# Keys by Strassen's seven products: a change to the shared-key stage of an mLSTM and band-attention trunk

## The chip, the cores and the metric

The kernel runs on one core of one Trainium2 chip. The metric is the device time of one execution in microseconds (us); lower is better. The core has five instruction queues that matter here: PE (the matrix engine), DVE (vector), ACT (scalar), POOL, which does next to nothing in this kernel, and SP, which only issues DMA transfers. Each queue takes its instructions in the order in which the program lists them, and an instruction that waits for a semaphore holds up everything behind it in its own queue.

## What is computed

The input is 512 tokens of width 2048, in float32. Layer A is an mLSTM mixer, layer B an attention mixer; both have a modulated RMSNorm ahead and a gated residual behind. Between the two layers one set of keys and values is computed from the residual stream, and layer B reads it. Cut to what the change touches:

```python
kmod = sc @ kv_ada_w.astype(F32) + kv_ada_b.astype(F32)
hkv = modulate(rmsnorm(x, kv_g), kmod[:, :D_MODEL], kmod[:, D_MODEL:]).astype(x.dtype)
kv = hkv @ kv_w                                            # 512 x 2048 by 2048 x 4096
k_sh = kv[..., :B_WIDTH].reshape(Bn, S, B_HEADS, B_DH)     # 16 heads of 128 features
v_sh = kv[..., B_WIDTH:].reshape(Bn, S, B_HEADS, B_DH)
...
def band_attention_mixer(h, k, v, w_in, rel_table, w_out):
    qz = h @ w_in
    q = qz[..., :B_WIDTH].reshape(Bn, S, B_HEADS, B_DH)
    z = qz[..., B_WIDTH:]
    o = chunk_band_attention(q, k, v, rel_table)
    y = o.reshape(Bn, S, B_WIDTH) * jax.nn.silu(z.astype(F32))
    return y.astype(h.dtype) @ w_out
```

## The kernel before

All arithmetic is float32, made of float32r matmuls. `split` writes a high part of an operand with ACT (the cast, L153) and the rest with DVE (the subtraction, L154), and `mm3` then issues three matmuls for each product: high by high, high by low, low by high (all at L174). So a 128x128 weight block against 512 tokens is three matmuls of 512 columns.

The weights (520 pieces of 512 KB and some smaller) are laid out in DRAM in the order in which they are used. `wpiece` takes the next one: a DMA on SP into a buffer `wr`, ACT's cast into `wh`, DVE's subtraction into `wl`. The pool `wp` holds three buffers of each kind. So the DMA of piece i+3 waits until DVE is through with piece i, and ACT's cast of piece i+3 waits until PE is through with piece i.

The program is written as Python loops, and a planner sets the order of the instructions on each engine; parts under `tc.high_priority(AHEAD)` (the weight pieces above all) are put forward. The order that comes out is fixed in the built program.

The stages in order: start and layer A (to 1544 us in the profile), A's output projection `ps_y` (to 1896), and then the part that the change is about:

- `residual` and `turned` finish the residual stream, turn it to features x tokens and keep it in the DRAM scratch `nsc`. `key_input` makes the 16 tiles `hkv` (128 features x 512 tokens, high and low), the input of the key and value projections.
- `values(g, ms)`: 512 columns of the values for the token tiles `ms`, accumulated in PSUM tiles `ps_kv`, then copied by ACT into the SBUF tiles `kv[h]`. The column groups g = 0 and 1 are done first for token tiles 0 and 1, then for 2 and 3 (`PAIRS`).
- the keys, a loop over 16 feature tiles: `proj_a` accumulates `ps_k` over 16 blocks of k (48 matmuls of 512 columns), ACT copies it into `kv[i]`.
- `values(2)` and `values(3)` on all four token tiles.
- 16 tiles `h2`, the input of layer B: each is read back from `nsc` (`kept`, into a tile `xt` of the pool `tp`, six buffers), scaled on DVE (L704) and split on ACT and DVE. They take the buffers of the `hkv` tiles, which come free one after another during `values(3)`.
- 16 heads: `queries`, `weights`, `gated`, `flipped`, `mixed`. Each head has two projections of 48 matmuls, `ps_q` and `ps_z`. `mixed` splits the gated output into a tile `y2`.
- the output projection of B on the 16 tiles `y2` (`ps_y` again), and `finish`.

Of the kernel before, what the change touches and what calls it, by code (L numbers as in the profile page):

```python
# [15 lines left out]
P = 128  # L16
# [24 lines left out]

def stream():

    out = []

    def tile_a(mat, col, kts=KT):
        for k in range(0, kts, 8):
            out.append((mat, list(range(k, k + 8)), [(col, P)]))

    def tile_b(mat, col, kts=KT):  # L50
        for k in range(0, kts, 2):
            out.append((mat, [k, k + 1], [(col, 512)]))

    for k0, k1 in BLOCKS:
        for k in range(k0, k1):
            out.append(("a_w_in", [k], [(c, P) for c in LEAD]))
        for c in LATER:
            out.append(("a_w_in", list(range(k0, k1)), [(c, P)]))
# [16 lines left out]
    for i in range(KT):  # L75
        tile_a("kv_w", i * P)
# [10 lines left out]


def sizes():
    return [len(kts) * sum(n for _, n in cs) for _, kts, cs in stream()]  # L90
# [15 lines left out]
def hybrid_trunk(ctx, tc, xT, xN, c, adaT, cols, wst, wg, ext, kc, out):  # L106
# [5 lines left out]
    wp = ctx.enter_context(tc.tile_pool(name="wp", bufs=3))  # L112
# [4 lines left out]
    def pool(name, bufs=1):  # L117
        return tc.tile_pool(name=name, bufs=bufs, reuse_waits="tile")
# [6 lines left out]
    bsc = dram.tile([BH, P, EXTW], F32, name="bsc")  # L125

# [31 lines left out]
    def wpiece(mat):  # L158

        i, at = wpos  # L160
        m, kts, cs = order[i]
        assert m == mat
        n = len(kts) * sum(w for _, w in cs)
        wpos[:] = i + 1, at + P * n
        with tc.high_priority(ahead[0]):
            raw = wp.tile([P, 1024], F32, tag="raw", name=f"wr{i}")[:, :n]
            nc.sync.dma_start(raw, wst[at : at + P * n].rearrange("(p n) -> p n", p=P))
            hi = wp.tile([P, 1024], F32R, tag="hi", name=f"wh{i}")[:, :n]
            lo = wp.tile([P, 1024], F32R, tag="lo", name=f"wl{i}")[:, :n]
            split(hi, lo, raw)  # L170
        return hi, lo
# [23 lines left out]
    def proj_b(mat, xs, pss, ms=range(4), kts=KT, at={}, late=0):  # L195
# [3 lines left out]
        for k0 in range(0, kts, 2):  # L199
# [14 lines left out]
            held.clear()  # L214

# [344 lines left out]
    kp = kst.enter_context(pool("kp", bufs=KT))  # L560
    rst = ExitStack()
    rp = rst.enter_context(pool("rp", bufs=12))
    tst = ExitStack()
    tp = tst.enter_context(pool("t2", bufs=6))
# [3 lines left out]
    def y_tile(k):  # L568
        while len(ys) <= k:
            h, q = divmod(len(ys) // 2, 2)  # L570
            with tc.high_priority(AHEAD):
                raw = wp.tile([P, 2, S], F32, tag="raw", name=f"yr{h}_{q}")
# [128 lines left out]
    for k in range(KT):  # L701
# [6 lines left out]
        h2.append(t)  # L708
    tst.close()
    rst.close()  # L710
# [4 lines left out]
    y2 = []  # L715

    def queries(h):
        ps = newp(f"ps_q{h}")
# [61 lines left out]
    def mixed(h, pts, v, sz):  # L780
# [29 lines left out]
    for m in range(4):  # L810
        t = [xp.tile([P, 2, S], F32, tag="x", name=f"x2_{m}_{i}") for i in range(2)]
# [25 lines left out]
    kst.close()  # L837


def layouts(x, c, ada_w, ada_b, g_pre, g_post, a_w_in, a_conv_w, a_conv_b, a_gate_b, a_g_head,  # L840
# [3 lines left out]
    def cc(v):  # L844
# [15 lines left out]
            np.concatenate([mats[mat][k * P : (k + 1) * P, c0 : c0 + n] for k in kts for c0, n in cs], 1).ravel()  # L860
# [32 lines left out]
```

## Time and profile before

| | us |
|---|---|
| median of 3 runs (lowest to highest) | 2863.78 (2862.81 to 2864.45) |
| the profiled execution's own time | 2862.53 |
| its span, from first to last instruction | 2860.7 |
| PE busy | 2832.2 (99%) |
| DVE busy | 1587.4 (55%) |
| ACT busy | 1126.1 (39%) |
| keys, `ps_k` (768 matmuls) | 174.08 |
| `values(2)` and `values(3)`, `ps_kv` (384 matmuls) | 87.04 |

The page gives for each engine its busy time; the chain of waits follows the end of the program back to what released each step; the timeline lists instructions by start and duration. A matmul's duration is its own passage through the array. What counts in a run of matmuls is the distance from one start to the next, which is shorter, since they overlap.

### The profile page before, as it was taken

The page shows a single profiled execution, that of the slowest core. Times are in us where ns is not written, and L with a number is a line of the kernel's source. Part 1 is how long each engine was busy: PE and PEld are TensorE (multiplying, and loading weights), DVE is VectorE, ACT ScalarE, POOL GpSimd, SP SyncE. Part 2 cuts the span into 40 slices and gives each one's busy share as a digit, 9 for nine tenths or more (in the row PEclk, how much of TensorE's full clock was granted, in tenths as well). Part 3 has the DMA queues.
Part 4 walks back from the last instruction along what each step waited for, and adds up shares of the span by engine and source line. Part 5 has one row for each costly group of instructions (what it writes and reads, how often), then busy time and mean ns, then how long its engine had stood idle before and what let it go on. Part 6 is the DMA issues. An engine that isn't in the chain of part 4 may idle for free.

```text
span 2860.7 us, 33028 instructions
## 1 busy us (share of the span) xinstructions
PE 2832.2 (99%) x12770; PEld 2340.4 (82%) x12770; DVE 1587.4 (55%) x2358; ACT 1126.1 (39%) x1646; POOL 0.2 (0%) x4
## 2 busy tenths in 40 slices
PE   7999999999999999999999999999999999999998
PEld 5787888888888888888888888888888888888887
DVE  7986747466375564764735445575222455545425
ACT  4244524333242342332424345454222445545323
POOL 0000000000000000000000000000000000000000
PEclk9999999999999999999999999999999999999999
DMA  8874546456456464554635557786222322222334
GB/s 307 310 235 159 192 158 211 168 173 209 155 184 213 136 225 155 195 203 154 209 108 177 180 195 238 231 274 217 96 99 103 138 92 86 90 91 88 137 103 173
DMA packets 154950, 491.09 MB, mean 172 GB/s; under 512 B 17012, under 2 KB 26132, under 8 KB 154280
## 3 DMA queue, kind: packets, MB, share of 16 engines
q1 hardware_dynamic: 154792, 488.98, 50.2%
q8 instruction: 100, 1.64, 0.2%
q14 instruction: 58, 0.48, 0.0%
HBM read 467.89 MB, written 26.26 MB: 173 GB/s over the span
## 4 chain that ended last, share of the span: by engine, by line
PE 93%; DVE 3%; DMA 2%; issue 1%; ACT 1%; SPq 0%; DVEq 0%; ACTq 0%
PE ps_y L174 17%; PE ps_z L174 17%; PE ps_o L174 12%; PE ps_v L174 12%; PE ps_qk L174 9%; PE ps_q L174 6%; PE ps_k L174 6%; PE ps_kv L174 5%; PE ps_l L174 2%; PE ps_s L174 2%; PE ps_n L174 2%; PE ps_lead L174 1%; DVE wl L154 1%; DVE ada L245 1%; DMA wr<-in_wst 1%
## 5 line engine op out<-in xcount | busy, mean ns | idle before, releaser
L154 DVE TENSOR_TENSOR wl<-wr,wh 128x1024 fp32r<-128x1024 f32 (+3 forms) x586 | 680.4, 1162 | 1078.1 <-ACT wh L153 1077.6
L153 ACT CAST wh<-wr 128x1024 fp32r<-128x1024 f32 (+3 forms) x586 | 587.3, 1003 | 1433.0 <-PE ps_y L174 235.6
L174 PE MATMUL ps_y<-wh,y 128*128 128x512 f32 x1536 | 475.2, 390 | 0.0
L174 PE MATMUL ps_z<-h,wh 128*128 128x512 f32 x1408 | 433.9, 389 | 0.0
L174 PEld LDWEIGHTS ps_y<-wh,y 128*128 128x128 f32 x1536 | 288.2, 188 | 59.2
L174 PE MATMUL ps_v<-wh,h 128*128 128x512 f32 x1024 | 317.2, 389 | 0.0
L174 PEld LDWEIGHTS ps_z<-h,wh 128*128 128x128 f32 x1408 | 263.3, 188 | 54.0
L174 PE MATMUL ps_y<-wl,y 128*128 128x512 f32 x768 | 299.1, 389 | 0.0
L174 PE MATMUL ps_o<-h,wh 128*128 128x512 f32 x896 | 276.2, 389 | 0.0
L174 PE MATMUL ps_z<-h,wl 128*128 128x512 f32 x704 | 274.1, 389 | 0.0
L174 PE MATMUL ps_qk<-h,wh 128*128 128x512 f32 x768 | 237.8, 391 | 0.0
L174 PEld LDWEIGHTS ps_v<-wh,h 128*128 128x128 f32 x1024 | 192.1, 188 | 39.8
L174 PE MATMUL ps_v<-wl,h 128*128 128x512 f32 x512 | 199.4, 390 | 0.0
L174 PEld LDWEIGHTS ps_o<-h,wh 128*128 128x128 f32 x896 | 167.3, 188 | 34.1
L245 DVE CUSTOM_DVE_ANT_0 ada<-ada,scB,mod 128x1024 f32<-128x1024 f32 x128 | 164.1, 1282 | 24.2 <-DMA ada<-in_adaT 22.7
L174 PE MATMUL ps_o<-h,wl 128*128 128x512 f32 x448 | 174.4, 389 | 0.0
L174 PEld LDWEIGHTS ps_y<-wl,y 128*128 128x128 f32 x768 | 144.2, 188 | 30.0
L245 DVE CUSTOM_DVE_ANT_0 ada<-ada,scB,cl 128x1024 f32<-128x1024 f32 x128 | 164.0, 1282 | 6.0 <-DMA ada<-in_adaT 5.9
L174 PEld LDWEIGHTS ps_qk<-h,wh 128*128 128x128 f32 x768 | 143.2, 188 | 29.1
L174 PE MATMUL ps_q<-h,wh 128*128 128x512 f32 x512 | 159.3, 392 | 0.0
L174 PE MATMUL ps_kv<-wh,hkv 128*128 128x512 f32 x512 | 159.2, 391 | 0.0
L174 PE MATMUL ps_k<-hkv,wh 128*128 128x512 f32 x512 | 157.5, 389 | 0.0
(216 smaller groups left out, 3389.0 us busy)
## 6 DMA issues: line engine op xcount, KB each, us to landing
wr<-in_wst SPq DMA_DIRECT2D x520, 512.0 KB, 3.3
ada<-in_adaT SPq DMA_DIRECT2D x256, 512.0 KB, 5.4
yr<-ysc SPq DMA_DIRECT2D x16, 512.0 KB, 3.6
wr<-in_wst SPq DMA_DIRECT2D x30, 256.0 KB, 4.5
ysc<-so SPq DMA_DIRECT2D x28, 256.0 KB, 5.3
wr<-in_wst SPq DMA_DIRECT2D x16, 384.0 KB, 5.4
bsc<-in_ext SPq DMA_DIRECT2D x16, 320.0 KB, 6.1
xt<-in_xT SPq DMA_DIRECT2D x4, 1024.0 KB, 7.0
```

The costliest lines, as they stand in the source:

```text
L153: nc.scalar.copy(hi, src)
L154: nc.vector.tensor_tensor(lo, src, hi.bitcast(F32), op=ALU.subtract)
L174: nc.tensor.matmul(ps, a, b, start=start, stop=stop)
L245: pin(nc.vector.tensor_tensor_reduce(at, at, scB[:, j * D // 2 : (j + 1) * D // 2], 1.0, mod[:, i : i + 1] if j else col(CB + i), ALU.mult ...
```

## The change

1. The keys are computed in eight pairs of feature tiles. Two feature tiles, two neighbouring k blocks and the two halves of the tokens (256 each) are a product of 2x2 blocks. Where the sums of the inputs are there, it is made with Strassen's seven block products (Winograd's form) in place of eight: seven times three matmuls of 256 columns in place of twelve of 512. `KEY_PAIRS` says for how many of the eight pairs of k blocks each feature pair does so: 4, 6, and then 8. The others are multiplied as before.
2. The weight sums are made in `wpiece`: three DVE additions on the loaded piece, which grows from 1024 columns to 1408 (one Strassen unit and one plain one) or 1792 (two units) before it is split. For this stage the weight pool is closed and opened again with larger buffers, three raw ones and two of each part in place of three (`weight_pool(3, 2)`), and it is opened once more with the old sizes ahead of layer B.
3. The input sums (`key_sums`, `half_sums`) are made from `nsc` again: two loads, two ACT scalings, four DVE additions and two splits for each pair of k blocks. Four of the eight are put into `values` of the second token pair, four into the first two feature pairs.
4. Each feature pair is taken out of four PSUM banks (D, C, A, B) by one ACT copy and five DVE additions.
5. Keys, values and gated outputs go to DRAM (`ksc`, `vsc`, `y2c`) in place of staying in SBUF. Values pass through a tile of the pool `tp`; each head fetches its keys and values one head ahead; the gated outputs are read back and split in the output projection.

```diff
+KEY_PAIRS = [4, 6, 8, 8, 8, 8, 8, 8]
+
+
+def pair_pieces(f):
+
+
+    sk, nk = list(range(f)), list(range(f, KT // 2))
+    n = min(len(sk), len(nk))
+    out = [([a], [b]) for a, b in zip(sk, nk)]
+    out[1:1] = [([], nk[i : i + 2]) for i in range(n, len(nk), 2)]
+    return out + [(sk[i : i + 2], []) for i in range(n, len(sk), 2)]
+
+
...
+    def tile_s(mat, c1, c2, f):
+        for sk, nk in pair_pieces(f):
+            blocks = [(2 * k + i, c, P) for i, c in ((0, c1), (0, c2), (1, c2), (1, c1)) for k in sk]
+            out.append((mat, blocks + [(2 * k + i, c, P) for k in nk for i in range(2) for c in (c1, c2)]))
...
-    for i in range(KT):
-        tile_a("kv_w", i * P)
+    for i in range(KT // 2):
+        tile_s("kv_w", 2 * i * P, (2 * i + 1) * P, KEY_PAIRS[i])
...
-    wp = ctx.enter_context(tc.tile_pool(name="wp", bufs=3))
     xp = ctx.enter_context(tc.tile_pool(name="xp", bufs=KT))
     psP = ctx.enter_context(tc.tile_pool(name="psP", bufs=5, space=bass.MemoryType.PSUM))
     psA = ctx.enter_context(tc.tile_pool(name="psA", bufs=3, space=bass.MemoryType.PSUM))
 
-    def pool(name, bufs=1):
-        return tc.tile_pool(name=name, bufs=bufs, reuse_waits="tile")
+    def pool(name, bufs=1, **kw):
+        return tc.tile_pool(name=name, bufs=bufs, reuse_waits="tile", **kw)
+
+    wst_ = ExitStack()
+    wps = []
+
+    def weight_pool(raw, parts):
+
+        wst_.close()
+        wps[:] = [wst_.enter_context(pool("wp", side="right")), raw, parts]
+
+    weight_pool(3, 3)
 
...
+    ksc = [dram.tile([P, 2, S], F32, name=f"ksc{i}") for i in range(BH // 2)]
+    vsc = [dram.tile([P, 4, S], F32, name=f"vsc{g}") for g in range(4)]
+    y2c = [dram.tile([P, 2, S], F32, name=f"y2c{i}") for i in range(BH // 2)]
 
...
+        wp, n_raw, n_parts = wps
         i, at = wpos
-        m, kts, cs = order[i]
+        m, blocks = order[i]
         assert m == mat
-        n = len(kts) * sum(w for _, w in cs)
+        n = sum(w for _, _, w in blocks)
         wpos[:] = i + 1, at + P * n
+        w = sk * P
+        size = 14 * P if wps[2] == 2 else 1024
         with tc.high_priority(ahead[0]):
-            raw = wp.tile([P, 1024], F32, tag="raw", name=f"wr{i}")[:, :n]
-            nc.sync.dma_start(raw, wst[at : at + P * n].rearrange("(p n) -> p n", p=P))
-            hi = wp.tile([P, 1024], F32R, tag="hi", name=f"wh{i}")[:, :n]
-            lo = wp.tile([P, 1024], F32R, tag="lo", name=f"wl{i}")[:, :n]
+            raw = wp.tile([P, size], F32, tag="raw", name=f"wr{i}", bufs=n_raw)[:, : n + 3 * w]
+            nc.sync.dma_start(raw[:, :n], wst[at : at + P * n].rearrange("(p n) -> p n", p=P))
+            hi = wp.tile([P, size], F32R, tag="hi", name=f"wh{i}", bufs=n_parts)[:, : n + 3 * w]
+            lo = wp.tile([P, size], F32R, tag="lo", name=f"wl{i}", bufs=n_parts)[:, : n + 3 * w]
+            if sk:
+                nc.vector.tensor_tensor(raw[:, n : n + 2 * w], raw[:, w : 3 * w], raw[:, : 2 * w], op=ALU.subtract)
+                nc.vector.tensor_tensor(raw[:, w : 2 * w], raw[:, n + w : n + 2 * w], raw[:, :w], op=ALU.add)
+                nc.vector.tensor_tensor(raw[:, n + 2 * w :], raw[:, 3 * w : 4 * w], raw[:, w : 2 * w], op=ALU.subtract)
             split(hi, lo, raw)
         return hi, lo
 
...
+    def proj_s(mat, xs, ss, f, z, name, at={}):
+
+
+        D, C, A, B = [newp(f"ps_{n}{name}") for n in "dcab"]
+        pieces = pair_pieces(f)
+        begun = set()
+        h0, h1_ = slice(0, 256), slice(256, 512)
+        for i, (sk, nk) in enumerate(pieces):
+            if i in at:
+                at[i]()
+            hi, lo = wpiece(mat, len(sk))
+            n = 4 * P * (len(sk) + len(nk))
+
+            def acc(ps, cols, w0, x, xcols, last):
+                start = id(ps) not in begun
+                begun.add(id(ps))
+                w = slice(w0, w0 + P)
+                mm3(ps[:, cols], hi[:, w], lo[:, w], x[:, 0, xcols], x[:, 1, xcols], start, last)
+
+            ns = len(sk)
+            nb = 4 * (ns + len(nk))
+
+            def eight():
+                for m, k in enumerate(nk):
+                    for j in range(2):
+                        for t, ps in enumerate((A, B)):
+                            acc(ps, slice(0, S), (4 * ns + 4 * m + 2 * j + t) * P, xs[2 * k + j], slice(0, S), False)
+
+            def seven():
+                end = i == len(pieces) - 1
+                for ps, cols, b0, x, xcols, last in (
+                    (D, h1_, ns, lambda k: ss[k][1], h0, False),
+                    (D, h0, 0, lambda k: xs[2 * k], h0, end),
+                    (C, h0, nb + ns, lambda k: ss[k][0], h1_, False),
+                    (C, h1_, nb, lambda k: ss[k][0], h0, end),
+                    (A, h0, 3 * ns, lambda k: xs[2 * k + 1], h0, False),
+                    (A, h1_, nb + 2 * ns, lambda k: xs[2 * k + 1], h1_, end),
+                    (B, h0, 2 * ns, lambda k: ss[k][1], h1_, end),
+                ):
+                    if i == 0 and ps is B:
+                        eight()
+                    for j, k in enumerate(sk):
+                        acc(ps, cols, (b0 + j) * P, x(k), xcols, last and j == ns - 1)
+
+            if i:
+                eight()
+            seven()
+        with tc.high_priority(AHEAD):
+            nc.scalar.copy(z[:, 0, :], D[:, h0])
+            nc.vector.tensor_tensor(z[:, 4, :], z[:, 0, :], D[:, h1_], op=ALU.add)
+            nc.vector.tensor_tensor(
+                z[:, 1:3, :], z[:, 4:5, :].to_broadcast([P, 2, 256]), C.rearrange("p (a t) -> p a t", a=2), op=ALU.add
+            )
+            nc.vector.tensor_tensor(z[:, 3, :], z[:, 1, :], C[:, h1_], op=ALU.add)
+            nc.vector.tensor_tensor(z[:, 0:2, :], z[:, 0:2, :], A.rearrange("p (a t) -> p a t", a=2), op=ALU.add)
+            if f < KT // 2:
+                nc.vector.tensor_tensor(z[:, 2:4, :], z[:, 2:4, :], B.rearrange("p (a t) -> p a t", a=2), op=ALU.add)
+            else:
+                nc.vector.tensor_tensor(z[:, 2, :], z[:, 2, :], B[:, h0], op=ALU.add)
+
+    def half_sums(raw, tmp, pl, tag, name):
+
+        (a11, a21), (a12, a22) = ((r[:, :256], r[:, 256:]) for r in raw)
+        (s1, s3), (s2, s4) = ((t[:, :256], t[:, 256:]) for t in tmp)
+        nc.vector.tensor_tensor(s1, a21, a22, op=ALU.add)
+        nc.vector.tensor_tensor(s3, a11, a21, op=ALU.subtract)
+        nc.vector.tensor_tensor(s2, a22, s3, op=ALU.subtract)
+        nc.vector.tensor_tensor(s4, a12, s2, op=ALU.subtract)
+        out = []
+        for i, t in enumerate(tmp):
+            s = pl.tile([P, 2, S], F32R, tag=tag, name=f"{name}_{i}")
+            split(s[:, 0, :], s[:, 1, :], t)
+            out.append(s)
+        return out
 
...
-    kv = [kp.tile([P, 2, S], F32, tag="k", name=f"kv{h}") for h in range(BH)]
-
     def values(g, ms, at={}):
         pv = [newp(f"ps_kv{g}_{m}") for m in ms]
         proj_b("kv_w", hkv, pv, ms=ms, at=at)
         for p, m in zip(pv, ms):
-            for j in range(4):
-                nc.scalar.copy(kv[4 * g + j][:, 1, m * P : (m + 1) * P], p[:, j * P : (j + 1) * P])
+            v = tp.tile([P, S], F32, tag="t", name=f"v{g}_{m}")
+            nc.scalar.copy(v, p)
+            nc.sync.dma_start(vsc[g][:, :, m * P : (m + 1) * P], v.rearrange("p (j t) -> p j t", j=4))
+
+    hs = []
+
+    def key_sums(k):
+        raw = [kept(2 * k + i, slice(0, S)) for i in range(2)]
+        for i, r in enumerate(raw):
+            c = KT + 2 * k + i
+            nc.scalar.activation(r, r, AF.Identity, bias=mod[:, 80 + c : 81 + c], scale=amul[:, c : c + 1])
+        tmp = [tp.tile([P, S], F32, tag="t", name=f"hs{k}_{i}") for i in range(2)]
+        hs.append(half_sums(raw, tmp, kp, "k", f"hs{k}"))
 
     with tc.high_priority(AHEAD):
         residual(2)
@@ -690,11 +811,20 @@
     for pair, ms in enumerate(PAIRS):
         for g in range(2):
             turn = {4 * i: lambda i=i: turned(1, [i], True) for i in range(4)} if pair == 0 and g == 1 else {}
+            if pair:
+                turn = {k: lambda k=k: key_sums(2 * g + k // 8) for k in (4, 12)}
             values(g, ms, turn)
-    for i in range(KT):
-        ps = newp(f"ps_k{i}")
-        proj_a("kv_w", hkv, ps)
-        nc.scalar.copy(kv[i][:, 0, :], ps)
+    rst.close()
+    zst = ExitStack()
+    zp = zst.enter_context(pool("zp", bufs=2))
+    weight_pool(3, 2)
+    for i in range(KT // 2):
+        z = zp.tile([P, 5, 256], F32, tag="z", name=f"zk{i}")
+        ready = len(hs)
+        at = {j: lambda: key_sums(len(hs)) for j in (1, 2)} if ready < KT // 2 else {}
+        assert ready == KEY_PAIRS[i]
+        proj_s("kv_w", hkv, hs, ready, z, f"k{i}", at)
+        nc.sync.dma_start(ksc[i].rearrange("p a t -> p (a t)"), z[:, 0:4, :].rearrange("p a t -> p (a t)"))
     for g in range(2, 4):
         values(g, range(4))
     h2 = []
...
+    zst.close()
     tst.close()
-    rst.close()
+    weight_pool(3, 3)
 
 
     ast = ExitStack()
     at = ast.enter_context(pool("att"))
-    y2 = []
+    kv = []
+
+    def fetch(h):
+        t = kp.tile([P, 2, S], F32, tag="k", name=f"kv{h}")
+        nc.sync.dma_start(t[:, 0, :], ksc[h // 2][:, h % 2, :])
+        nc.sync.dma_start(t[:, 1, :], vsc[h // 4][:, h % 4, :])
+        kv.append(t)
+
+    fetch(0)
 
     def queries(h):
+        if h < BH - 1:
+            fetch(h + 1)
         ps = newp(f"ps_q{h}")
         proj_a("b_w_in", h2, ps)
         q0 = at.tile([P, P], F32, tag="q0", name=f"q0_{h}")
...
-        t = kp.tile([P, 2, S], F32R, tag="k", name=f"y2_{h}")
-        split(t[:, 0, :], t[:, 1, :], sz)
-        y2.append(t)
+        nc.sync.dma_start(y2c[h // 2][:, h % 2, :], sz)
 
     qs, ptv, szs = {}, {}, {}
     for h in range(BH + 2):
...
+    y2 = []
+
+    def y2_tile(k):
+        while len(y2) <= k:
+            i = len(y2) // 2
+            with tc.high_priority(AHEAD):
+                raw = wps[0].tile([P, 2, S], F32, tag="raw", name=f"y2r{i}", bufs=wps[1])
+                nc.sync.dma_start(raw, y2c[i])
+                for j in range(2):
+                    t = xp.tile([P, 2, S], F32R, tag="x", name=f"y2_{i}_{j}")
+                    split(t[:, 0, :], t[:, 1, :], raw[:, j, :])
+                    y2.append(t)
+        return y2[k]
 
...
-            proj_b("b_w_out", y2, ps, ms=pair, at=at, late=3 if pair == PAIRS[1] else 0)
+            proj_b("b_w_out", y2_tile, ps, ms=pair, at=at, late=3 if pair == PAIRS[1] else 0)
```

More of the change, by code (lines that the diff above doesn't have):

```diff
@@ L86, in stream @@
     return out
-def sizes():
-    return [len(kts) * sum(n for _, n in cs) for _, kts, cs in stream()]
 CB = 0
@@ L560, in hybrid_trunk @@
     kp = kst.enter_context(pool("kp", bufs=KT))
+    tst = ExitStack()
+    tp = tst.enter_context(pool("t2", bufs=6))
     rst = ExitStack()
     rp = rst.enter_context(pool("rp", bufs=12))
-    tst = ExitStack()
-    tp = tst.enter_context(pool("t2", bufs=6))
     ys = []
@@ L571, in y_tile @@
             with tc.high_priority(AHEAD):
-                raw = wp.tile([P, 2, S], F32, tag="raw", name=f"yr{h}_{q}")
+                raw = wps[0].tile([P, 2, S], F32, tag="raw", name=f"yr{h}_{q}", bufs=wps[1])
                 nc.sync.dma_start(raw, ysc[h, :, 2 * q : 2 * q + 2, :])
@@ L810, in hybrid_trunk @@
     for m in range(4):
-        t = [xp.tile([P, 2, S], F32, tag="x", name=f"x2_{m}_{i}") for i in range(2)]
+        t = [kp.tile([P, 2, S], F32, tag="k", name=f"x2_{m}_{i}") for i in range(2)]
         for i in range(2):
@@ L837, in hybrid_trunk @@
     kst.close()
+    wst_.close()
 def layouts(x, c, ada_w, ada_b, g_pre, g_post, a_w_in, a_conv_w, a_conv_b, a_gate_b, a_g_head,
@@ L859, in layouts @@
         [
-            np.concatenate([mats[mat][k * P : (k + 1) * P, c0 : c0 + n] for k in kts for c0, n in cs], 1).ravel()
-            for mat, kts, cs in order
+            np.concatenate([mats[mat][k * P : (k + 1) * P, c0 : c0 + n] for k, c0, n in blocks], 1).ravel()
+            for mat, blocks in order
         ]
```

12 lines of the change are left out of this document (7 added, 5 removed).

## The prediction

> **What bounds the kernel now.** I read the page's busy times and chain of waits first: PE carries the end, and what is not PE on the chain is small.
>
> ```profile
> PE 2832.2 (99%) x12770; PEld 2340.4 (82%) x12770; DVE 1587.4 (55%) x2358; ACT 1126.1 (39%) x1646; POOL 0.2 (0%) x4
> PE 93%; DVE 3%; DMA 2%; issue 1%; ACT 1%; SPq 0%; DVEq 0%; ACTq 0%
> ```
>
> Then the chain in order of time (start, duration, matmuls) around the keys. The rows join without a gap: each stage ends where the next begins, and PE has never waited here.
>
> ```profile
> 1989.28 174.08 PE ps_k L174 x768
> 2163.36 87.04 PE ps_kv L174 x384
> 2250.40 10.88 PE ps_q L174 x48
> 2261.28 10.88 PE ps_z L174 x48
> ```
>
> So a matmul of 512 columns costs 174.08 / 768 = 0.2267 us, and any PE work saved here is saved in the end, as long as PE stays fed. For 256 columns I read the timeline of the mLSTM scores, where six of them stand together.
>
> ```profile
> 516.40 0.88 PE L174 MATMUL ps_s<-qk,qk 128*128 128x256 f32 x6
> 517.11 0.63 PE L174 MATMUL ps_o<-h,wh 128*128 128x512 f32 x2
> ```
>
> From their start to the next matmul is 0.71 us, so 0.118 each; other heads give 0.118 to 0.125. I take 0.120. Third, what feeds PE: the split of a weight piece, the making of an `h2` tile (L704, then L153 and L154), their loads with the time from issue to landing, two other loads that bound it, and SP's longest wait (us in total, times, longest).
>
> ```profile
> L154 DVE TENSOR_TENSOR wl<-wr,wh 128x1024 fp32r<-128x1024 f32 x520 | 636.4, 1224 | 1072.0 <-ACT wh L153 1071.5
> L153 ACT CAST wh<-wr 128x1024 fp32r<-128x1024 f32 x520 | 547.7, 1053 | 1330.8 <-PE ps_y L174 235.6 <-PE ps_z L174 228.0 <-PE ps_v L174 153.6
> L704 DVE TENSOR_SCALAR xt<-xt,amul,mod 128x512 f32<-128x512 f32 x16 | 8.5, 544 | 8.4 <-DMA xt<-nsc 8.4
> L154 DVE TENSOR_TENSOR h<-xt,h 128x512 fp32r<-128x512 f32 x16 | 11.0, 687 | 3.5 <-ACT h L153 3.5
> L153 ACT CAST h<-xt 128x512 fp32r<-128x512 f32 x16 | 10.0, 623 | 7.8 <-PE ps_kv L174 7.8
> wr<-in_wst SPq DMA_DIRECT2D x520, 512.0 KB, 3.3
> xt<-nsc SPq DMA_DIRECT2D x16, 256.0 KB, 3.4
> bias<-bsc SPq DMA_DIRECT2D x16, 256.0 KB, 2.6
> ada<-in_adaT SPq DMA_DIRECT2D x256, 512.0 KB, 5.4
> SPq L167 <- DVE wl L154: 1776.1, 510, 11.2
> ```
>
> SP stands in one order and waits at an issue for its buffer; whatever is listed behind that issue waits with it. Last, what an idle PE costs besides the idle time.
>
> ```profile
> 29.14 2.50 PE L174 MATMUL ps_lead<-h,wh 128*128 128x512 f32 x5 [3.42 <-ACT h L224]
> 31.43 0.63 PE L174 MATMUL ps_lead<-h,wl 128*128 128x512 f32 x1
> 31.86 0.63 PE L174 MATMUL ps_lead<-h,wh 128*128 128x512 f32 x1
> ...
> 66.51 1.43 PE L174 MATMUL ps_lead<-h,wh 128*128 128x512 f32 x5 [2.63 <-ACT h L224]
> 67.77 0.39 PE L174 MATMUL ps_lead<-h,wl 128*128 128x512 f32 x1
> 68.00 0.39 PE L174 MATMUL ps_lead<-h,wh 128*128 128x512 f32 x1
> ```
>
> After 3.42 us of idling the matmuls start 0.43 us apart until 34.4, twelve of them, 12 x 0.2 = 2.4 us lost; after 2.63 us they start 0.23 apart.
>
> **A. The products: -11.6 us.** A Strassen unit takes 7 x 3 matmuls of 256 columns, 21 x 0.120 = 2.52 us, in place of 12 x 0.2267 = 2.72. `KEY_PAIRS` sums to 58 units: 58 x 0.20 = 11.6 us. The keys' own matmuls come to 1218 x 0.120 + 72 x 0.2267 = 162.5 us. Bounds by the rows: 0.118 gives -14.0, 0.125 gives -5.5.
>
> [...]
>
> **B. Entering the keys: +6.7 us.** In the order in which the changed program, once built, lists its instructions on each engine, SP issues the first key piece (434) only behind the store of the values v1_2, which waits for ACT's copy, which waits for one of the last matmuls of the values. Before, pieces came three buffers ahead. Counted from the end of the last value matmul: v1_2's last matmul ends at -1.2, copy 0.58, store and issue of 434 at -0.2, landing +3.3 = 3.1. Three weight sums on DVE (256, 128 and 128 columns: 0.42 + 0.28 + 0.28) to 4.1; ACT's cast of 1408 columns, 1.38 on the line through 1024 (1.05) and 768 (0.84), to 5.5. PE restarts there and does seven small matmuls (0.84) without the low parts. The sums of piece 435 stand ahead of the low part of 434 on DVE; 435 lands some 1.8 us after 434, so that goes from 5.9 to 7.55 (1408 columns: 1.62). Idle 7.55 - 0.84 = 6.7. With landings of 2.6 and 5.4 it is 6.0 and 8.8.
>
> **C. The first two feature pairs: +2.4 us.** Two `key_sums` are in each pair. On DVE one is 4 x 0.42 + 2 x 0.69 = 3.1 us. Added up in the built order, with the sums (0.98 a piece) and splits (1.62), DVE keeps up until pair 0 has to be taken out of its banks: piece 438's low part is ready 28.2 after the end of the values, and bank C is free (third of the five DVE additions that empty pair 0) at 31.4, where `ps_ak1` waits for it. PE wants it at about 29.1. So piece 438 ends near 35.3, where the five pieces so far need 26.2; 6.7 of that difference is B, 2.4 is C. A cold restart after B (up to 2.4 us by the row above) goes into the same wait: PE later, less to wait. Bounds: 0, if DVE runs ahead by 2 us; 4.8, if the cold stretch adds to it.
>
> **D. Pairs 3 to 8: nothing.** A piece holds two units, 5.04 us of PE. With two buffers the loop is: PE leaves piece i, ACT casts 1792 columns (1.70), DVE subtracts (2.02), 3.8 in all. DVE has 1.53 + 2.02 for each piece and about 2.9 to empty a pair, 17.1 of 20.2 us. The cover is 1.3 us a piece; without it each of 24 pieces would pay.
>
> **E. Leaving the keys: +0.5 us.** `values(2)` needs four banks within 2 us of its start; the last one it gets, A, is emptied 2.5 after the end.
>
> **F. Entering layer B: +15 us, the largest term.** Before, the 16 `h2` tiles were loaded and split during `values(3)`. Now values and `h2` share the six buffers of `tp`, and SP lists the `h2` loads behind the stores of the last values: store v3_2, pieces 482 to 484, store v3_3, xt0, pieces 485 to 487, then xt1 and on. Piece 485 waits for the low part of 482, 486 for 483, 487 for 484. Behind 487 all of `h2` but its first tile waits, and PE waits for `h2`. From the last value matmul:
> - 482 is issued at -0.2 and lands at 3.1, 483 and 484 at 4.7 and 6.2 (512 KB every 1.6 us). ACT 1.05, DVE 1.22 each: low parts done at 5.4, 7.0, 8.5.
> - xt0 then takes 0.54 + 0.62 + 0.69; PE does its first matmul at 9.7, six in all.
> - xt1 is issued at 8.9, lands at 12.3, and its low part is done at 14.2. DVE then needs 0.54 + 0.69, with the handing over 1.3 us, for each tile: `h2` 7 at 22.0.
> - The low parts of 485 and 486 (2 x 1.22) and eight tiles more (8 x 1.23): 34.3. PE has 11 matmuls left, 2.5 us: 36.8.
> Before, the same 96 matmuls took 21.8. The loss is 15.0. PE itself has 90 matmuls left at 13.5, 20.4 us and 2.4 for a cold start, to 36.3, so DVE just sets the end. Landings of 2.6 and 5.4, twice in this chain, give 13.5 and 19.2; I widen the low end to 11, since DVE might need no 0.07 for handing over and PE's last eleven be fewer.
>
> [...]
>
> **G. What else moves: +1 us.** 96 more DMAs: 16 stores of values, 16 loads for the sums, 8 key stores, 32 fetches, 16 and 8 for the gated outputs. During the second pair of values DMA goes from 200 to about 280 GB/s (the 37 us from 1763 ran at 293 with 0.24 us of PE idle), DVE to 73%. In the heads a split leaves (0.69 DVE, 0.62 ACT) and nothing on PE's path comes. Ahead of the output projection DVE gains four splits less one, 2.1 us, where it stood idle from 2666.2 to 2669.9. I take 1 for all, 0 to 4.
>
> **Sum.** -11.6 + 6.7 + 2.4 + 0.5 + 15.0 + 1 = +14.0 us on the profiled execution (2862.53). The median of the runs stands 1.25 higher, 2863.78, so 2877.8: I say 2878. All low ends together are -14 + 6 + 0 + 0 + 11 + 0 = +3, all high ends -5.5 + 8.8 + 4.8 + 1 + 19.2 + 4 = +32.
>
> **Rivals.**
> 1. *Faster: PE is fed through both hand-overs.* A, E and G alone would be left, -10.1: 2854. For it: before, PE has no wait at either place. Against it: the issue orders in B and F. It decides if xt1 is issued 13 us before the last value matmul rather than 9 behind it.
> 2. *Nearly level: half of F is hidden.* If pieces 483 and 484 land with 482 and DVE runs ahead, F falls to 7 and B to 5, +4.3 in all: 2868.
> 3. *The split loop binds.* If sums or emptying stand ahead of the low part in each piece, 3.8 + 1.5 passes 5.04 by 0.3, x 24 = +7: 2885.
> 4. *Weight loads bind.* A load's own duration is 0.188 us (PEld), longer than 0.120. In the burst of six their starts are 0.127 apart; sustained, 1218 x 0.007 = +8.5: 2886. At 0.188 it were +83, which the burst excludes.
>
> **How the numbers follow.** Forecast 0.66 (its own range 2869 to 2889), rival 1 0.08, rival 2 0.10, rival 3 0.10, rival 4 0.06. The range 2863 to 2891 leaves out rival 1 and the outer ends of the others. A change of 0.2% is 5.7 us, about what a measurement can tell: faster is rival 1 (0.08); level is most of rival 2 (0.08); slower 0.84.
>
> **What would show it.** `ps_d`, `ps_c`, `ps_a`, `ps_b` of 256 columns 0.12 us apart; the stage between the value groups some 172 us where it was 174; PE idle 5 to 7 us ahead of `ps_dk0` and near 10 us ahead of the first `ps_q`, then waits for `h2` on DVE until about 37 us behind the values; heads of 26.7 us as before. I am wrong if `h2` loads land during the values, if `ps_q` starts at once, or if the small matmuls run at another pace.

## The result, and the profile after

The changed kernel takes 2882.22 us (median of 4 runs, 2881.55 to 2884.36); the kernel before took 2864.07 beside it (2862.81 to 2864.45). The ratio is 1.0065, with a 95% interval from 1.0048 to 1.0083: 18 us slower. The forecast was 2878, with a range from 2863 to 2891.

The page of the changed kernel, its busy times and the shares of its chain of waits:

```profile
PE 2829.5 (98%) x13292; PEld 2359.0 (82%) x13292; DVE 1688.4 (59%) x2542; ACT 1156.5 (40%) x1622; POOL 0.2 (0%) x4
PE 90%; DVE 4%; DMA 2%; issue 1%; ACT 1%; SPq 0%; DVEq 0%; ACTq 0%
```

PE is busy for 2.7 us less than before, and its share of the chain falls from 93% to 90%. More is lost in waiting than is gained in work. The chain in order of time (start, duration, matmuls) shows where:

```profile
1990.87 4.45 DMA wr<-in_wst
...
2032.12 1.44 PE ps_dk L211 x12
...
2163.16 85.72 PE ps_kv L211 x378
2251.25 6.17 DMA wr<-in_wst
2260.15 4.59 DMA xt<-nsc
...
2289.99 10.88 PE ps_q L211 x48
```

Before, the stages joined here without a gap and every row was PE's. Now each of the two hand-overs has the landing of a DMA on it, the second one two, one behind the other. Twelve matmuls of 256 columns in 1.44 us are the 0.120 apiece that the sum rests on.

The stages follow from the first matmul of each in the timelines of PE (head 1 is counted as 10.88 us, its 48 matmuls of `ps_q`, ahead of the first `ps_s`):

| stage, us | before | after | difference | forecast |
|---|---|---|---|---|
| up to the first value matmul | 1896.62 | 1897.15 | +0.5 | G |
| `values` 0 and 1 | 92.50 | 93.66 | +1.2 | G |
| from there to `values(2)`: the keys | 174.08 | 172.19 | -1.9 | A, B, C, D, E: -2.0 |
| `values` 2 and 3 | 87.04 | 87.07 | 0.0 | 0 |
| from there to head 1 | 21.76 | 39.76 | +18.0 | F: +15 |
| head 1 to the first `ps_y` | 397.66 | 397.90 | +0.2 | G |
| first `ps_y` to the last group of `ps_o` | 18.12 | 19.93 | +1.8 | G |
| the rest | 172.92 | 172.74 | -0.2 | G |

The five rows of G come to 3.5, where 1 was forecast. At the hand-overs PE's timeline has these rows (what stands in brackets is the idle time ahead of the row and what ended it):

```profile
1997.92 0.79 PE L211 MATMUL ps_dk<-hs,wh 128*128 128x256 f32 x2 [6.96 <-ACT wh L182]
...
2022.81 0.47 PE L211 MATMUL ps_ak<-hkv,wh 128*128 128x256 f32 x2 [0.26 <-DVE zk L306]
...
2163.00 0.40 PE L211 MATMUL ps_kv<-wh,hkv 128*128 128x512 f32 x1
...
2260.90 1.52 PE L211 MATMUL ps_q<-h,wh 128*128 128x512 f32 x2 [10.68 <-ACT h L182]
...
2266.01 0.80 PE L211 MATMUL ps_q<-h,wh 128*128 128x512 f32 x1 [1.88 <-ACT h L182]
```

Counting a matmul as 0.227 us from its start, as above, the last one of the second value pair ends at 1990.81 and that of `values(3)` at 2250.07 (the brackets count from the end of its passage, some 0.16 later). So PE stands for 7.1 us ahead of the keys, hardly at all ahead of `ps_ak1` and not at all ahead of `values(2)`; ahead of layer B it stands for 10.8 us and, six matmuls later, for 1.9 more. SP's timeline (start, time from the first issue to the last, tiles) says why:

```profile
2246.80 3.23 SPq L796 DMA_DIRECT2D vsc<-v  x3
2250.20 1.49 SPq L200 DMA_DIRECT2D wr<-in_wst  x3
2251.74 0.52 SPq L796 DMA_DIRECT2D vsc<-v  x1
2252.30 0.68 SPq L762 DMA_DIRECT2D xt<-nsc  x1
2256.54 3.56 SPq L200 DMA_DIRECT2D wr<-in_wst  x3
2260.15 8.27 SPq L762 DMA_DIRECT2D xt<-nsc  x8
```

The three first weight pieces of layer B go out behind three of the four stores of the last values, the next three only as the low parts of the first three are done, and behind these stands all of `h2` but its first tile, 10 us after PE ran out of work. And when PE begins, it is at half its clock. The view by windows (length, busy time and matmuls of PE, then of the other engines, and the granted clock of PE) of the first 15 us:

```profile
2260.90:2266.00 5.10, 3.23 (x6) 1.78 (x6) 1.36 (x3) 0.62 (x1) 0.00 (x0) 0.50 0.93 309
2266.00:2271.90 5.90, 5.89 (x14) 4.30 (x15) 5.90 (x12) 3.26 (x6) 0.00 (x0) 0.50 0.78 275
2271.90:2276.00 4.10, 4.10 (x19) 3.38 (x18) 3.44 (x7) 1.07 (x2) 0.00 (x0) 1.00 0.77 259
```

Twenty matmuls run at 0.50 of the clock and the next at 1.00. PE has work without a stop from 2266.01 on.

### The profile page after: what moved, and what is told of

It is laid out like the page before. It is cut to its first block, busy times and chain, and to the rows that moved or that the text cites. A ratio compares the mean times of both kernels' runs of the same rounds, so it can differ in the third digit from the quotient of the medians.

```text
span 2880.4 us, 34450 instructions
## 1 busy us (share of the span) xinstructions
PE 2829.5 (98%) x13292; PEld 2359.0 (82%) x13292; DVE 1688.4 (59%) x2542; ACT 1156.5 (40%) x1622; POOL 0.2 (0%) x4
## 4 chain that ended last, share of the span: by engine, by line
PE 90%; DVE 4%; DMA 2%; issue 1%; ACT 1%; SPq 0%; DVEq 0%; ACTq 0%
PE ps_y L211 17%; PE ps_z L211 16%; PE ps_v L211 12%; PE ps_o L211 12%; PE ps_qk L211 9%; PE ps_q L211 6%; PE ps_kv L211 5%; PE ps_s L211 2%; PE ps_n L211 2%; PE ps_ak L211 2%; DMA wr<-in_wst 2%; PE ps_l L211 1%; PE ps_dk L211 1%; PE ps_ck L211 1%; DVE ada L357 1%
## 5 line engine op out<-in xcount | busy, mean ns | idle before, releaser
L183 DVE TENSOR_TENSOR wl<-wr,wh 128x1024 fp32r<-128x1024 f32 (+4 forms) x586 | 703.2, 1201 | 976.3 <-ACT wh L182 975.7
L182 ACT CAST wh<-wr 128x1024 fp32r<-128x1024 f32 (+4 forms) x586 | 605.5, 1034 | 1379.7 <-PE ps_z L211 277.2
L211 PEld LDWEIGHTS ps_z<-h,wl 128*128 128x128 f32 x704 | 132.4, 188 | 27.8
```

Of the source, the lines that this page charges most:

```text
L182: nc.scalar.copy(hi, src)
L183: nc.vector.tensor_tensor(lo, src, hi.bitcast(F32), op=ALU.subtract)
L211: nc.tensor.matmul(ps, a, b, start=start, stop=stop)
```

## Experiments

The theory in question: the products save what was forecast, and the loss is two waits that come from the order of the transfers, with a slow PE behind each. All kernels are edits of the changed one. Median and ratio go by the runs of the kernel before on the same chip; the three stages (keys, from the values to head 1, first `ps_y` to last `ps_o`) are those of the table above, each from one profiled execution.

| kernel | us | before beside it | ratio, 95% | keys | to head 1 | to last `ps_o` |
|---|---|---|---|---|---|---|
| changed | 2882.22 | 2864.07 | 1.0065 (1.0048 to 1.0083) | 172.19 | 39.76 | 19.93 |
| e1 stores on ACT | 2871.19 | 2863.85 | 1.0029 (1.0018 to 1.0040) | 167.86 | 35.23 | 20.59 |
| e2 values apart from `h2` | 2871.36 | 2863.85 | 1.0025 (1.0015 to 1.0035) | 171.63 | 28.72 | 18.84 |
| e3 both | 2865.96 | 2863.85 | 1.0005 (0.9995 to 1.0014) | 168.25 | 28.58 | 19.12 |
| e4 PE kept busy | 2879.18 | 2863.85 | 1.0055 (1.0040 to 1.0070) | 172.02 | 40.47 | 19.21 |
| e5 keys as before | 2890.51 | 2863.53 | 1.0095 (1.0079 to 1.0110) | 182.13 | 39.98 | 19.01 |
| e6 `y2` not put forward | 2879.12 | 2863.53 | 1.0054 (1.0040 to 1.0067) | 171.96 | 39.62 | 18.31 |
| e7 SP and ACT free | 2863.78 | 2863.53 | 1.0001 (0.9992 to 1.0010) | 166.92 | 26.33 | 19.47 |
| e8 PE kept busy longer | 2879.37 | 2863.53 | 1.0057 (1.0043 to 1.0071) | 174.20 | 38.72 | 19.07 |
| e9 e7, busy, and e6 | 2859.85 | 2863.45 | 0.9987 (0.9978 to 0.9995) | 165.33 | 24.69 | 18.31 |
| e10 e9, sums on POOL | 2872.03 | 2863.45 | 1.0032 (1.0020 to 1.0044) | 175.34 | 24.70 | 18.31 |

### e1: the stores leave SP

```diff
-            nc.sync.dma_start(vsc[g][:, :, m * P : (m + 1) * P], v.rearrange("p (j t) -> p j t", j=4))
+            nc.scalar.dma_start(vsc[g][:, :, m * P : (m + 1) * P], v.rearrange("p (j t) -> p j t", j=4))
```

> Changed kernel with one edit: the 16 stores of the values are issued by ACT in place of SP. Theory (PE idles at both hand-overs because the loads of the first weight pieces stand on SP behind stores that wait for the last value matmuls): piece 434 and 482 are then issued more than 5 us ahead of the end of their value stages. Entering the keys PE idles about 2.6 us in place of 7.1 (ACT still copies v1_3 and issues its store ahead of the cast of 434: 0.6 + 0.5 + 1.4), and the cold stretch (1.9) goes: -6.4. Entering layer B the first ps_q starts some 7.0 behind the values in place of 10.8; the h2 loads behind piece 487 still come late, so only that shift of 3.7 is won. Sum 2882.2 - 10.1 = 2872 (2868 to 2877). Rival 1 (the landing itself is slow, 4.5 us under the crowd of transfers, not the place in the queue): both waits stay within 1 us, 2880 to 2882. Rival 2 (DVE cannot empty feature pair 0 in time): PE idles again ahead of ps_ak1, up to 4.8 us given back, 2877.

The total came out 1 below the 2872. The list of PE's waits of this kernel (us in all, times, longest):

```profile
PE ps_q L211 <- ACT h L182: 8.9, 2, 5.9
...
PE ps_dk L211 <- ACT wh L182: 2.7, 1, 2.7
```

Ahead of the keys PE waits 2.7 for the forecast 2.6; so the place behind the stores made the wait, and rival 1 is out. Of the 6.4 forecast for the keys 4.3 came: PE was slow again after this shorter wait (0.21 us from one matmul of 256 columns to the next until 1999.2), and waited 0.6 ahead of `ps_ak1` where it had been 0.26. Entering layer B 4.5 came, where 3.7 was forecast.

### e2: the last values leave the buffers of `h2`

```diff
-            v = tp.tile([P, S], F32, tag="t", name=f"v{g}_{m}")
+            if g < 2:
+                v = tp.tile([P, S], F32, tag="t", name=f"v{g}_{m}")
+            elif m % 2 == 0:
+                zv = zp.tile([P, 5, 256], F32, tag="z", name=f"v{g}_{m}").rearrange("p a t -> p (a t)")
+                v = zv[:, :S]
+            else:
+                v = zv[:, S : 2 * S]
```

> Changed kernel with one edit: values(2) and values(3) pass through the two buffers of zp in place of tp, so that tp's six buffers are the h2 loads' own. Theory (h2 comes late because its tiles share tp with the last value tiles): 14 of the 16 h2 tiles are made during values(3), as before the change. The first ps_q then waits for piece 482 alone: issued at the end of the values, landing after 4 us, cast 1.05: PE idles 5.2 in place of 10.8, is cold for 1 to 2 us, and does the 96 matmuls in 21.8 without a further wait. From the last value matmul to head 1 about 29.5 in place of 39.8, the keys unchanged: 2882.2 - 10.3 = 2872 (2869 to 2874). Rival (the wait for the first weight pieces carries the whole loss, h2 is covered by it): 2880 to 2882. Rival (the h2 loads in values(3) crowd out weight pieces): PE waits within values(3), longer than 87.1, and less than 5 is won.

11.0 was won between the values and head 1, where 10.3 was forecast, and `values(2)` and `values(3)` still take 87.07: making `h2` beside them costs nothing. PE's first wait is 4.8 (5.2 forecast), with one of 0.2 behind it; the slow clock takes the rest of the 2.0 that are left above the 21.76 of the matmuls. The larger part of F is `h2`, and it is late because its tiles share buffers with the last values.

### e3: both

No further edit.

> Both edits together. Theory: the two causes add. Keys as with the first edit, -6.4. Entering layer B piece 482 is there early and h2 too; ACT still has two copies and two store issues ahead of the cast: first ps_q 3.4 us behind the values, head 1 at 25 to 27 in place of 39.8, -13.5. Sum 2882.2 - 19.9 = 2862 (2858 to 2866), level with the kernel before (2864.1) or just below. Rival (a third wait sets the hand-overs, such as bank release): less than 14 in all, 2868 or more.

2866.0, the top of the range, level with the kernel before. At both hand-overs less was won than forecast: 3.9 of 6.4 in the keys, and head 1 at 28.6 rather than 25 to 27. The gains of e1 and e2 do not simply add: to head 1 it takes no less than in e2, although PE's first wait falls from 4.8 to 2.8. The shorter wait is followed by a second one of 0.5 for the low part and by a longer slow stretch: PE is back at its full clock 10.4 behind the values, in e2 8.6.

### e5: the keys as before, all else changed

```diff
...
-        proj_s("kv_w", hkv, hs, ready, z, f"k{i}", at)
-        nc.sync.dma_start(ksc[i].rearrange("p a t -> p (a t)"), z[:, 0:4, :].rearrange("p a t -> p (a t)"))
+        zr = z.rearrange("p a t -> p (a t)")[:, :S]
+        ps = newp(f"ps_k{i}")
+        proj_a("kv_w", hkv, ps)
+        nc.scalar.copy(zr, ps)
+        nc.sync.dma_start(ksc[i // 2][:, i % 2, :], zr)
```

The loop has 16 feature tiles again, with the weight pieces laid out as before, and no `key_sums` is made.

> Changed kernel with the keys multiplied as before the change (16 tiles of 48 matmuls of 512 columns, no sums), all else left: keys, values and gated outputs in DRAM, the same pools, the same order of the stages. Theory (Strassen's products save 11.6 and their own DVE work costs 2 to 3, the loss is all in the hand-overs): PE idles 5.5 ahead of the keys (landing 4.4, cast 1.05) and is cold for 2, so the stage takes 174.1 + 7.5 = 181.6 in place of 172.2; into layer B 39.8 as in the changed kernel. Sum 2882.2 + 9.4 = 2891.6 (2888 to 2894). Rival (what the seven products save, their sums take back): 2884 or less.

The keys take 182.1, as forecast, with 5.4 of waiting ahead of them, and the way to head 1 is the same 40.0. So the seven products are worth 9.9 us in the stage, sums and emptying included (the medians of the two kernels are 8.3 apart), and the move to DRAM by itself, with its pools, would have cost 27.

### e4 and e8: PE kept busy at the hand-overs

```diff
+    def warm(a, b, n):
+
+        ps = newa("ps_warm")
+        for i in range(n):
+            mm(ps, b[1][:, 0, :P], a[0][:, 0, :], True, True)
...
+    warm(hs[0], hs[1], 30)
     rst.close()
...
+    warm(hs[6], hs[7], 46)
     h2 = []
```

> Changed kernel with matmuls added that nobody reads: 30 of 512 columns ahead of the keys, 46 ahead of layer B, where PE stands idle for 7.1 and 10.8 us. Nothing else is moved. Theory (behind a long idle PE runs at half pace, and this and not DVE sets the end of the stage into layer B): the keys' 256-column matmuls start 0.12 apart at once, 1.9 saved; into layer B the first matmuls start 0.23 apart, piece 482 is let go earlier, ACT casts 485 earlier, and head 1 comes 2 us earlier (1.5 to 2.5). Sum 2882.2 - 3.9 = 2878.3. Rival of the prediction (DVE, making h2 tiles, sets the end): head 1 unchanged, 2880.3. Rival (the slow stretch has another cause than idling): matmuls behind the added ones still 0.21 and 0.43 apart, 2882.

The total fell by 3.0 of the forecast 3.9, but the profile does not carry it (its execution was the slowest of the four, 2882.8), and neither stage gained there; where the 3.0 come from stays open. In the keys the matmuls did start 0.12 apart at once, but now PE waited for DVE: 0.45 for the low part of piece 434, 0.25 and 0.71 for the banks of pair 0, and the stage took 172.0 as before. On the way to head 1 the six matmuls were over sooner, `h2` 1 landed 1.7 us later after its issue, PE stood for 4.9, and was slow again, 0.43 us from one matmul of 512 columns to the next. So e8 had the second row of added matmuls end with the arrival of `h2` 1:

```diff
-    warm(hs[6], hs[7], 46)
+    warm(hs[6], hs[7], 66)
```

> The kernel with added matmuls once more, 66 in place of 46 ahead of layer B (30 ahead of the keys as there): PE is busy until 15.0 behind the values, and h2 1, which nothing of this moves, came at 15.9 to 17.3. So PE has no long wait left in which to get cold. Theory (the slow stretch behind an idle PE lengthens the stage): the first matmuls of ps_q and ps_z start 0.23 apart, and head 1 comes 20.4 behind h2 1, at 36.5 to 37.7 in place of 39.8; total 2879.5. Rival of the prediction (DVE, making 16 h2 tiles and two low parts, sets the end whatever PE does): PE waits for h2 several times and head 1 stays at 39 or later.

```profile
2271.43 0.50 PE L211 MATMUL ps_q<-h,wh 128*128 128x512 f32 x1 [0.91 <-ACT h L182]
2272.16 0.50 PE L211 MATMUL ps_q<-h,wh 128*128 128x512 f32 x1 [0.22 <-DVE h L183]
```

These are PE's only waits between the last value matmul and head 1, both for `h2` 1. From there, at 16.7 behind the values, to head 1 at 38.7 PE does 93 matmuls in 22.0 us; in the changed kernel it does 90 in 23.8. So with PE at full clock (0.23 from one matmul to the next) DVE still keeps up, and what set the end was the arrival of `h2` 1 and PE's own work, part of it slow. At 38.7 head 1 lies between the theory (at most 37.7) and the rival (39 or later), and it is the missing waits for later `h2` tiles that speak against the rival. Head 1 came 1 us later than forecast, since `h2` 1 was later by 0.8 than in the changed kernel and PE found three matmuls to do ahead of it in place of six. The total, 2879.4, is the forecast 2879.5, but again the profile does not carry it (2884.4, the slowest of the four): in it the keys took 2.0 longer than in the changed kernel, with four waits for DVE of 0.3 to 0.7 and a stretch of 3.4 at half the clock (0.83 granted on the mean from 2020 to 2030).

### e6: the reads of the gated outputs

```diff
-            with tc.high_priority(AHEAD):
+            with tc.high_priority(0):
                 raw = wps[0].tile([P, 2, S], F32, tag="raw", name=f"y2r{i}", bufs=wps[1])
                 nc.sync.dma_start(raw, y2c[i])
```

> Changed kernel, the gated outputs' reads and splits put forward by no priority where the output projection begins. Theory (the stretch from the first ps_y to the last ps_o is 1.8 longer than before because the splits of y2 stand ahead of head 15's steps on ACT and DVE): that stretch falls from 19.9 to 18.1 or 18.6, the total to 2880.7 (2879.5 to 2881.5). Rival (the reads are then late for the projection): PE waits for y2 in the projection, 2883 or more.

In the changed kernel PE has one wait in this stretch, 0.74 at 2691.93 ahead of `ps_t` of head 15, for DVE's low part of `pt`; ACT's cast for it stands behind two casts of `y2`. In e6 the stretch falls to 18.3, and PE has no wait in it. The same 18.31 comes in e9 and e10, which have this edit too; in the eight kernels without it, it is 18.8 to 20.6. So the place of the `y2` splits on ACT and DVE, ahead of head 15's steps, costs 0.5 to 2.3, in the changed kernel 1.6 of its 1.8. The total fell by 3.1, to 2879.1, just below the forecast range; what is over 1.6 this edit does not explain.

### e7, e9 and e10: can the products be kept and the waits removed?

e7 takes e2's buffers, and gives neither SP nor ACT anything to do for `values(2)` and `values(3)`:

```diff
-            nc.scalar.copy(v, p)
-            nc.sync.dma_start(vsc[g][:, :, m * P : (m + 1) * P], v.rearrange("p (j t) -> p j t", j=4))
+            (nc.scalar.copy if g < 2 else nc.vector.tensor_copy)(v, p)
+            nc.gpsimd.dma_start(vsc[g][:, :, m * P : (m + 1) * P], v.rearrange("p (j t) -> p j t", j=4))
```

> Changed kernel with three edits: values(2) and values(3) through zp's buffers, all 16 stores of the values issued by POOL's queue, and the copies of values(2) and values(3) made by DVE, so that neither SP nor ACT has anything of the values between the last value matmul and the first weight piece. Theory: entering the keys PE idles 2.0 (v1_3's copy 0.6, cast 1.4), the stage takes 167.2; into layer B the cast of 482 ends 1.7 behind the values, its low part 2.9, so that PE idles 2.1 in all, head 1 at 24.5 (24 to 26) in place of 39.8. From the 2866.0 of both edits alone: -0.8 - 4.1 = 2861 (2858 to 2863), faster than the kernel before (2863.9). Rival (a wait of DVE, for h2 or for the copies, takes the place): head 1 at 28 or later, 2865 or more.

The total, 2863.8, misses the range (2858 to 2863) and is level with the kernel before. The keys are at the forecast (166.9 for 167.2); the way to head 1 is 1.8 longer. The view by windows of e7 (PE's busy time and matmuls, granted clock, DMA share, GB/s) shows it, first at the keys and then at layer B:

```profile
1992.48:1994.63 2.15, 0.16 (x1) 1.00 0.99 378
1994.63:1998.10 3.47, 3.47 (x15) 0.51 0.54 165
...
2248.28:2250.82 2.54, 1.83 (x7) 0.97 0.83 241
2250.82:2254.17 3.35, 3.35 (x10) 0.51 0.96 287
```

The waits are near the forecast (2.15 for 2.0; 1.8 and 0.7 more for the low part, for 2.1), and yet PE falls to half its clock after each, for 3.4 us; at layer B not at once but 2.5 us after it began. So e9 fills the two waits with twelve matmuls each and takes e6's edit:

```diff
+    warm(hs[0], hs[1], 12)
     rst.close()
...
+    warm(hs[6], hs[7], 12)
     h2 = []
```

> The three edits of the kernel before this one (level with the unchanged kernel: keys 166.9, head 1 at 26.3 behind the values), with twelve unread matmuls (2.7 us) at each of the two hand-overs, and the gated outputs' reads put forward by no priority. Theory: PE does not get cold, head 1 comes at 2.7 + 21.8 + 0.3 = 24.8; in the keys DVE takes back what the clock gives, as the longer row of added matmuls showed, so 166.5; the stretch from the first ps_y to the last ps_o 18.3 to 18.8 in place of 19.5. Sum 2863.8 - 0.4 - 1.5 - 0.9 = 2861 (2859 to 2863). Rival (the short waits, 2.2 and 1.8, leave the clock alone, and the matmuls only fill the time): 2864.

2859.85, 3.6 us below the kernel before, which was measured beside it: of the kernels here the one whose interval lies wholly below 1. But 0.13% is less than the 0.2% that the prediction named as what can be told from no change. Head 1 at 24.7 is the forecast 24.8. The keys gained more than forecast: 165.3 is the 2.7 of the added matmuls, 162.5 of the keys' own, and 0.1. No wait for DVE is left. That DVE takes back what the clock gives was so in e4, where the first piece was issued late; in e9 it was not.

e10 had been put beside it for that case:

```diff
-        nc.vector.tensor_tensor(s1, a21, a22, op=ALU.add)
+        nc.gpsimd.tensor_tensor(s1, a21, a22, op=ALU.add)
```

and so for the other three additions of `half_sums`.

> The same with the 32 additions of the input sums (128x256, eight key_sums) on POOL in place of DVE. Theory (in the first two feature pairs DVE is what PE waits for): DVE is relieved of 3.4 us in each of the two pairs, the waits for the emptied banks go, and the keys take 162.5 of matmuls and 3.3 of hand-over, 165.8 or less; total 0.7 to 1.5 below the kernel beside it. Rival (POOL takes much longer than DVE's 0.42 for an addition, or DVE slows beside it, and the sums come too late): keys 167 or more, the total above the kernel beside it.

The rival holds: 10 us longer in the keys, 4.1 in the values ahead. One group, first of e9 on DVE, then of e10 on POOL (busy time, mean ns):

```profile
L320 DVE TENSOR_TENSOR hs<-xt,hs 128x256 f32<-128x256 f32 x8 | 3.4, 424 | 0.2
```

```profile
L320 POOL TENSOR_TENSOR hs<-xt,hs 128x256 f32<-128x256 f32 x8 | 10.5, 1317 | 0.6
```

The four additions take 794 to 1317 ns on POOL in place of 0.42 us, and in the same stretch DVE's subtraction of 1024 columns goes from 1220 ns to 1341. So an addition of 256 columns took 1.9 to 3.1 times as long on POOL as on DVE.

## Why the prediction was right, and where its steps were off

**A, the products, -11.6: right.** 0.120 us for 256 columns all through the stage, 5.04 us for each piece of two units. e5 puts the stage 9.9 apart, of which the two hand-overs' own difference (5.6 against 7.1 of idling, 2.4 against 2.6 behind it) takes 1.6 from the 11.6.

**B and C, entering the keys, +9.1, and E, +0.5: right in sum, off in their parts.** Measured: 7.1 of idling, 1.9 of slow matmuls (20 between 1997.92 and 2002.29), 0.7 of the rest, 9.7 in all. In B the landing took 4.45 where the median of 3.3 had been taken, so PE began 7.1 behind the values rather than 5.5; but the low part, priced as a second wait, was covered, because the seven matmuls ahead of it ran slowly, at 0.50 of the clock. In C the wait for bank C was 0.26, and the cold restart stood in its place. The prediction had the cold restart go "into the same wait", and e4 shows that so it is: without the cold restart DVE's waits come instead. E did not come at all: `values(2)` follows the last key matmul without a gap.

**D, pairs 3 to 8, nothing: right.** The pieces of the full pairs follow each other at 5.04 us. Rivals 3 and 4, which would have lengthened every piece, are out.

**F, entering layer B, +15: right in its mechanism, mis-sized by 3.0.** Each step of its chain is in SP's rows. Two terms were short. The first was "lands at 3.1": the landings were some 1.1 later, that of `xt1` 4.6 behind an issue already 1.2 later, so that `h2` 1 let PE go on at 15.9 where "PE itself has 90 matmuls left at 13.5": 2.4. The second was "2.4 for a cold start": 14 matmuls at half pace and small gaps, 3.4. And "so DVE just sets the end", at 36.8 where PE alone would be at 36.3, is the wrong end of that step. DVE made a tile in 1.06 and not in 1.3, it waited for ACT for 2.0 in the middle, since ACT's cast of 485 waited for PE to let 482 go; and e8, with PE at full clock, has no wait for any `h2` behind `h2` 1. e2 shows the larger cause to be the shared buffers, e1 the smaller to be the stores on SP.

That a cold start is priced at all rests on two rows, 3.42 us of idling with half the pace behind it (0.43 us a matmul) and 2.63 without (0.23). Read as a length that is safe, the second was luck of that execution: the same wait at the same place, 2.60 to 2.72 us, is followed by half the clock in six of the other eleven kernels. The last section shows what it went with.

**G, the rest, +1: low by 2.5.** The heads are as forecast (+0.2). The failed step is the output projection: "DVE gains four splits less one, 2.1 us, where it stood idle" took a gap in DVE's time for cover, but the splits have casts on ACT ahead of them and stand ahead of the steps of head 15, for which PE waits. e6 gives 1.6 of it back. The 1.2 in the first values and the 0.5 ahead of them were not tested. The 0.5 says nothing: up to the first value matmul the changed kernel and the ten experiments take 1895.5 to 1900.0, in a part that none of the edits touches. Of the 1.2, 0.7 is one wait of PE for ACT's cast of a weight piece (at 1914.33, ahead of the first store of the values), which is 0 to 1.8 in the experiments. These take 93.0 to 97.7 for the first values, more than the 92.5 of before in each of them, e5 too, which makes no input sums. The 280 GB/s that G expected in the second pair of values did not come: 230, where the kernel before has 229.

**The rivals.** Rival 1 needed `xt1` to be issued 13 us ahead of the last value matmul. That was not so, and e9 shows what its mechanism is worth: fed through both hand-overs but for 2.7 us at each, and with e6's edit, the kernel is 3.6 below the one before, where rival 1 had 10 below. Rival 2 (pieces landing together, DVE ahead) did not happen: the landings were later, not closer.

## What to carry to other kernels

When a stage is made cheaper, look first at its two ends: what is issued ahead of it, on which queue, behind what wait, and whose buffers it shares. Here 10 us of saved work cost 27 us, nearly all at the hand-overs, because loads stood in one queue behind stores of the stage before, and all but 3 us at each of them came back by giving the stores another queue, the last copies another engine, the loads their own buffers, and PE something to do. And a gap in an engine's busy time is cover only if nothing behind it in that engine's order is being waited for, as the 1.6 us that e6 won back show.

## What the runs showed of the hardware

- In these traces every change of PE's granted clock lies on marks 3.413 us apart, and the marks lie elsewhere from one execution to the next (one is at 61.74 in the kernel before, one at 64.12 in e2). In the changed kernel the clock is at half from 1995.36 to 2002.19 and from 2254.78 to 2271.85, 2 and 5 times 3.413 long, and the second stretch begins 76 times 3.413 behind the first. In all twelve kernels each stretch at half the clock is a whole multiple of this length, but for the one that the end of the trace cuts off.
- In these traces the fall to half the clock goes not with the length of a wait but with how much idling falls between two marks. All twelve kernels have the same wait of 2.60 to 2.72 us near the start. Two of them, cut at their marks (length, busy time and matmuls of PE, clock, DMA share, GB/s), first the kernel before, then e2:

```profile
61.74:65.16 3.42, 2.13 (x10) 1.00 1.02 390
65.16:68.57 3.41, 2.06 (x9) 1.00 1.00 374
...
64.12:67.53 3.41, 1.01 (x4) 1.00 0.97 344
67.53:70.95 3.42, 3.42 (x9) 0.50 1.03 381
```

A mark splits the wait of the kernel before into 1.28 and 1.35, and the clock stays; in e2 2.4 of it lie between two marks, and the next 3.41 us run at half. From the first mark that the traces show on (32 to 35 us), 25 stretches at full clock between two marks hold 1.99 us of idling or more, over all twelve kernels, and half the clock follows each of them; of the others, with 1.81 or less, three were followed by it (1.73, 1.42 and 0.42 of idling). The clock came back behind the first stretch with less than 0.45 of idling, and never behind one with more than 0.55. So in these runs it was the place of the marks that decided whether a wait of 2 us cost a slow stretch: in e7 the 1.99 us ahead of the keys did, and so did 1.0 of the 1.65 at layer B with the 0.70 behind it, 2.4 us after PE had started again.

- The same load took 4.6 us from issue to use in one kernel and 6.3 to 6.4 in two others (`xt1`, the load for `h2` 1, in the changed kernel, in e1 and in e4), each time right behind three pieces of 512 KB.
